# Aligning the programs of ACT and DVE to 128 rows, in an add and GELU kernel

## The chip, the cores and the metric

The kernel runs on one NeuronCore of one Trainium2 chip. The metric is the device time of one execution in microseconds (us), median of several runs, with a granted clock of 1.0. Each run also lists its span, the time from the first to the last instruction that the trace records. Time and span are not the same: the time takes in something that the span does not, and the difference of the two, 2.2 us here, is "the time outside the span".

Engines: in the traces SP issues all 11 DMA transfers; POOL (GpSimd), DVE (VectorE) and ACT (ScalarE) compute, with 19, 35 and 34 instructions. "Row" is one instruction of one engine's program.

## The reference

```python
x, y: 1024 x 4096 float32
z = x + y
out = 0.5 * z * (1 + np.tanh(np.sqrt(2 / np.pi) * (z + 0.044715 * z ** 3)))
```

The kernel computes the second line as z * sigmoid(2 * sqrt(2/pi) * (z + 0.044715 z^3)).

## The kernel before

Each of 128 partitions holds 32,768 elements of z. They are loaded in 4 pieces of x and 4 of y, computed in 16 chunks of 2,048, and stored in 3 pieces.

```python
loads = [8192, 8192, 8192, 8192]
stores = [16384, 10240, 6144]
...
add(c):  POOL (DVE for c = 0)   z = z + y
sq(c):   ACT   w = Square(root * z)          # w in PSUM
stt(c):  DVE   w = (w + c1) * z
sig(c):  ACT   w = Sigmoid(w)
mul(c):  DVE   z = w * z
```

Two helpers edit the finished program. One moves the first two loads ahead of the barrier of all engines with which the program begins; the other makes only POOL wait for the last store at the end, after two closing barriers.

```python
def begin_early(nc, count):
    ...
    at = next(k for k, i in enumerate(head.instructions) if i.engine == SP and isinstance(i, mybir.InstDrain))
    for k, i in enumerate(moved):
        body.instructions.remove(i)
        head.instructions.insert(at + k, i)
...
    tc.compile()
    begin_early(nc, 2)
    wait_late(nc)
```

In the trace of the kernel before, the first row of ACT and of DVE is a drain (at 0.13 and 0.12 us, 8 and 10 ns long), their part in the first barrier; the rows of a program are counted from there. ACT has 55 such rows and DVE 45.

Of the kernel before, what the change touches and what calls it, by code (L numbers as in the profile page):

```python
# [10 lines left out]
def begin_early(nc, count):  # L11


    blocks = nc.main_func.blocks
    head, body = blocks[0], blocks[1]
    SP = mybir.EngineType.SP
    queue = [i for i in body.instructions if i.engine == SP]
    moved = [i for i in queue if isinstance(i, mybir.InstDMACopy)][:count]
    assert not any(i.sync_info and i.sync_info.on_wait for i in moved)
    at = next(k for k, i in enumerate(head.instructions) if i.engine == SP and isinstance(i, mybir.InstDrain))  # L20
    for k, i in enumerate(moved):
        body.instructions.remove(i)
        head.instructions.insert(at + k, i)


def wait_late(nc):


    body, end = nc.main_func.blocks[1:3]
    SP, POOL = mybir.EngineType.SP, mybir.EngineType.Pool  # L30
    last = [i for i in body.instructions if isinstance(i, mybir.InstDMACopy)][-1]
    (sem,) = [u.id for u in last.sync_info.on_update]
    all_done = end.instructions[0]
    clear = next(i for i in end.instructions if isinstance(i, mybir.InstDrain) and i.is_reset_sema)
    assert all_done.engine == SP and clear.engine == POOL and clear.sync_info is None
    waits = all_done.sync_info.on_wait
    its = [w for w in waits if w.id == sem]
    assert len(its) == 1
    rest = [w for w in waits if w.id != sem]

    def drain(old, waits, **reset):
        return mybir.InstDrain(
            name=old.name, engine=old.engine, debug=old.debug,
            sync_info=mybir.SyncInfo(on_wait=waits, on_update=[]), **reset
        )

    at = end.instructions.index(clear)
    clears = [
        drain(
            clear, its, is_reset_sema=True,  # L50
            reset_range_start=clear.reset_range_start, reset_range_stop=clear.reset_range_stop,
        ),
        end.instructions[at + 1],
    ]
    assert isinstance(clears[1], mybir.InstISA) and clears[1].engine == POOL
    del end.instructions[at : at + 2]
    end.instructions[0] = drain(all_done, rest, is_reset_sema=False)
    end.instructions.extend(clears)
# [3 lines left out]
def kernel(  # L62
# [14 lines left out]
    nc = tc.nc  # L77
# [144 lines left out]
    tc.close()  # L222
    tc.compile()  # L223
    begin_early(nc, 2)
    wait_late(nc)


# [28 lines left out]
```

## Time and profile before

| | kernel before |
|---|---|
| time, median of 6 runs | 121.09 us (121.03 to 121.23) |
| span | 118.9 us |
| time outside the span | 2.2 us |
| data in and out | 50.33 MB, DMA queue busy 98.6% |
| first data, last data | 1.02 us, 118.25 us |
| busy DVE, ACT, POOL | 62%, 51%, 59% |

The 16 DMA engines carry data 98.6% of the time, so the end of the span follows the last data. Each transfer is 128 packets of equal size and completes in 16 parts, taken here as one for each DMA engine; the trace records when each part completes. For the last store all 16 completed between 118.33 and 118.69 us. The part that is furthest behind sets the end: it completed at 118.69 us, and the last two rows of the trace, POOL's, follow at 118.71 and 118.82 us.

One line of the timeline, the first add on DVE, which waits for the first loads (start, duration, engine, line, operation, shapes, and the wait before it):

```profile
21.84 2.29 DVE L145 TENSOR_TENSOR z<-z,y 128x2048 f32<-128x2048 f32 x1 [20.44 <-DMA y<-in_y_dram]
```

### The profile page before, as it was taken

The numbers are of one execution on the slowest core, as the hardware profiler recorded it, in microseconds if no ns is written. First come the engines' busy times: TensorE is split into PE (matmuls) and PEld (weight loads), VectorE is DVE, ScalarE is ACT, GpSimd is POOL, SyncE is SP. The second block draws the span as 40 slices with busy tenths as digits, with TensorE's granted clock in tenths as the row PEclk, the third lists the DMA queues.
The fourth block names the chain that finished last, engine by engine and source line by source line (L and its number), as shares of the span: only waits on it lengthen the run. The fifth ranks groups of instructions, "written<-read, shape, count | busy, mean of one in ns | idle before, by whom it ended". The sixth has DMA issues, their size and how long they took to land.

```text
span 118.9 us, 170 instructions
## 1 busy us (share of the span) xinstructions
DVE 73.7 (62%) x35; ACT 61.0 (51%) x34; POOL 69.7 (59%) x19
## 2 busy tenths in 40 slices
DVE  0000000635799995749999958999994999990000
ACT  4000000064888865197698657888829769800000
POOL 0000000699995199999959999959999990000000
DMA  7989898989999898989899998998898889999996
GB/s 254 452 364 518 353 529 353 518 364 474 408 430 452 364 518 353 529 353 518 364 474 408 408 474 353 529 529 353 353 683 375 353 353 441 441 441 441 397 397 265
DMA packets 1584, 50.33 MB, mean 423 GB/s; under 512 B 176, under 2 KB 176, under 8 KB 176
## 3 DMA queue, kind: packets, MB, share of 16 engines
q1 hardware_dynamic: 1584, 50.33, 98.6%
HBM read 33.55 MB, written 16.78 MB: 423 GB/s over the span
## 4 chain that ended last, share of the span: by engine, by line
DMA 51%; POOL 26%; POOLq 4%; DVE 4%; DVEq 2%; ACT 2%; issue 0%; SPq 0%
DMA y<-in_y_dram 51%; POOL z L145 26%; POOLq L223 4%; DVE w L156 2%; DVEq L223 2%; DVE z L168 2%; ACT w L150 2%; SPq L121 0%; POOLq L145 0%
## 5 line engine op out<-in xcount | busy, mean ns | idle before, releaser
L145 POOL TENSOR_TENSOR z<-z,y 128x2048 f32<-128x2048 f32 x15 | 69.4, 4661 | 28.2 <-DMA y<-in_y_dram 28.2
L150 ACT ACTIVATE w<-z 128x2048 f32<-128x2048 f32 x16 | 30.1, 1882 | 37.6 <-DVE z L145 21.4
L156 DVE SCALAR_TENSOR_TENSOR w<-w,z 128x2048 f32<-128x2048 f32 x16 | 36.7, 2295 | 11.2 <-ACT w L150 11.0
L168 DVE TENSOR_TENSOR z<-w,z 128x2048 f32<-128x2048 f32 (+1 forms) x17 | 35.9, 2155 | 0.0
L161 ACT ACTIVATE w<-w 128x2048 f32<-128x2048 f32 x16 | 29.7, 1855 | 4.4 <-DVE w L156 4.3
L145 DVE TENSOR_TENSOR z<-z,y 128x2048 f32<-128x2048 f32 x1 | 2.3, 2292 | 20.4 <-DMA y<-in_y_dram 20.4
L208 ACT ACT_TABLE_LOAD x1 | 1.3, 1283 | 1.3 <-PEq L240 1.3
L207 DVE MEMSET one<- 128x1 f32 x1 | 0.1, 59 | 1.3 <-PEq L240 1.3
L240 POOL MEMSET const-float32-0.0<- 128x1 f32 x1 | 0.1, 99 | 0.2 <-issue 0.2
L208 ACT ACTIVATE one<-one 128x1 f32<-128x1 f32 x1 | 0.2, 203 | 0.0
L240 POOL MEMSET const-bfloat16-1.0<- 128x1 bf16 x1 | 0.1, 101 | 0.0
L240 POOL MEMSET const-uint8-127<- 128x1 uint8 x1 | 0.1, 101 | 0.0
L240 POOL MEMSET const-float32-1.0<- 128x1 f32 x1 | 0.1, 98 | 0.0
## 6 DMA issues: line engine op xcount, KB each, us to landing
z<-in_x_dram SPq DMA_DIRECT2D x4, 4096.0 KB, 31.3
y<-in_y_dram SPq DMA_DIRECT2D x4, 4096.0 KB, 22.2
out_dram<-z SPq DMA_DIRECT2D x1, 5120.0 KB, 15.8
out_dram<-z SPq DMA_DIRECT2D x1, 3072.0 KB, 11.9
out_dram<-z SPq DMA_DIRECT2D x1, 22.0
```

Of the source, the lines that this page charges most:

```text
L145: eng.tensor_add(out=zt[:, a:b], in0=zt[:, a:b], in1=yt[s][:, o : o + b - a])
L150: nc.scalar.activation(out=wt[c], in_=zt[:, a:b], func=act.Square, scale=root)
L156: nc.vector.scalar_tensor_tensor(out=wt[c], in0=wt[c], scalar=c1, in1=zt[:, a:b], op0=alu.add, op1=alu.mult)
L161: nc.scalar.activation(out=wt[c], in_=wt[c], func=act.Sigmoid)
L168: ins = nc.vector.tensor_mul(out=zt[:, a + o : a + o + n], in0=wt[c][:, o : o + n], in1=zt[:, a + o : a + o + n],)
L207: nc.vector.memset(one, 0.0)
L208: nc.scalar.activation(out=one, in_=one, func=act.Sigmoid)
L223: tc.compile()
L240: nc = _bacc.Bacc("TRN2", target_bir_lowering=False, num_devices=1)
```

## The change

The trace of the kernel before has six packets of kind "instruction", of 8,192 bytes each, 11.3 to 8.5 us ahead of the span. I read them as parts of the engines' programs, and call such a packet a fetch; what it holds is not shown. The alignment of the diff is to 128 rows. A "block" below is such a run of 128 rows, a "slot" the place of one row in it, a "border" the place between two of them. That a packet brings just such a block is not shown. A program that starts in the middle of a block may run over a border. The change pads the programs of ACT and DVE so that each begins at a border, to keep the whole program within one block.

```diff
+def align_start(nc):
+    head = nc.main_func.blocks[0].instructions
+    tail = nc.cur_bb.bb.instructions
+    for eng in (nc.scalar, nc.vector):
+        eng.addr_align(128)
+        ins = tail.pop()
+        at = next(
+            k for k, i in enumerate(head)
+            if i.engine == ins.engine and isinstance(i, mybir.InstDrain)
+        )
+        head.insert(at, ins)
...
     begin_early(nc, 2)
+    align_start(nc)
     wait_late(nc)
```

## The prediction

> **What bounds the kernel now.** I read the page first, then the DMA queue by stretches, then the timeline of the start and the waits of the SP queue. The page gives the transfers the whole span:
>
> ```profile
> DMA  7989898989999898989899998998898889999996
> ...
> q1 hardware_dynamic: 1584, 50.33, 98.6%
> ...
> z<-in_x_dram SPq DMA_DIRECT2D x4, 4096.0 KB, 31.3
> y<-in_y_dram SPq DMA_DIRECT2D x4, 4096.0 KB, 22.2
> ```
>
> The busy digits of the 16 DMA engines hardly leave 8 to 9 from the first slice to the last but one, and the queue's packets fill 98.6% of the engines' time. 50.33 MB is 3 x 16.78 MB: x in, y in, the result out, each once, so no byte can be saved by a change like this. By stretches (columns: window and length, busy time of DVE, ACT and POOL with instruction counts, clock, DMA share, GB/s) the first and last two rows are:
>
> ```profile
> 0.00:1.02 1.02, 0.00 (x0) 0.00 (x0) 0.20 (x4) 1.00 0.00 0
> 1.02:11.00 9.98, 0.06 (x1) 1.49 (x2) 0.00 (x0) 1.00 1.04 420
> ...
> 109.00:118.30 9.30, 0.00 (x0) 0.00 (x0) 0.00 (x0) 1.00 0.95 409
> 118.30:118.90 0.60, 0.00 (x0) 0.00 (x0) 0.00 (x0) 1.00 0.00 0
> ```
>
> Nothing moves in the first 1.02 us (SP issues the first load at 0.00, data follows about 1.02 us later), then data flows until about 118.3 us, then 0.6 us of completion and clearing. So the span of 118.9 us is 1.0 + 117.3 + 0.6, and the middle term is 50.33 MB at 429 GB/s. The timed 121.06 us has another 2.2 us outside the span. The chain of waits on the page names POOL for 26%, but it ends with the last multiply at 106.7 us, before the last store; it is not what sets the end. What sets it is whether the queue ever runs dry. It does not: the last load's data is in at 80.0 us and the first store was issued at 77.3; that store is in at about 99.3 and the second was issued at 95.7; that one is in at 111.4 and the third was issued at 106.8. The slacks are 2.7, 3.6 and 4.6 us.
>
> The start is where the change acts:
>
> ```profile
> 0.00 0.38 SPq L121 DMA_DIRECT2D z<-in_x_dram  x1
> ...
> 0.43 0.42 SPq L128 DMA_DIRECT2D y<-in_y_dram  x1
> 1.26 1.28 ACT L208 ACT_TABLE_LOAD   x1 [1.26 <-PEq L240]
> 1.26 0.33 SPq L121 DMA_DIRECT2D z<-in_x_dram  x1
> 1.33 0.06 DVE L207 MEMSET one<- 128x1 f32 x1 [1.33 <-PEq L240]
> ```
>
> The two first loads go out before the barrier of all engines, which releases at about 1.2 us; the third load is the first thing on SP after it. ACT and DVE then do tiny set-up work and wait for data:
>
> ```profile
> DVE z L145 <- DMA y<-in_y_dram: 20.4, 1, 20.4
> ACT w L150 <- DVE z L145: 21.4, 1, 21.4
> ```
>
> [...] its packet records hold six packets of kind "instruction" of 8,192 bytes[...]. They took 455 to 549 ns each and all ran 11.3 to 8.5 us ahead of the span. The windows view of that time shows them (12 GB/s in 4 us is 49 KB) and none between them and the start:
>
> ```profile
> -12.00:-8.00 4.00, 0.00 (x0) 0.00 (x0) 0.00 (x0) 1.00 0.05 12
> -8.00:-1.00 7.00, 0.00 (x0) 0.00 (x0) 0.00 (x0) 1.00 0.00 0
> -1.00:0.00 1.00, 0.00 (x0) 0.00 (x0) 0.00 (x0) 1.00 0.00 0
> ```
>
> In the span the packet records hold no instruction packet. [...]
>
> **The change part by part.** It removes nothing. It adds one alignment per program (ACT, DVE), ahead of the drain with which the engine enters the first barrier; the listing of the two programs shows one more row on each of the two engines and no other row moved. Rows of POOL, SP and PE are the same.
>
> (1) Padding. The alignment has to skip up to 127 slots. [...] the event semaphores of this trace took 17 ns on ACT and 21 ns on DVE[...]. Where SP runs several in a row they start some 60 ns apart (107.155 and 107.219 us). So 127 of them are 2.2 to 2.7 us at the least and 127 x 0.06 = 7.6 us at the most; on average half. ACT and DVE pad at the same time. An estimate, for the real number of slots is not in the trace.
>
> (2) What that delays. The barrier would release at up to 1.2 + 7.6 = 8.8 us, and with it the third load, the table load (1.28 us) and the memset. The third load needs to be out 1.02 us before the first two are through, at 21.7 us: slack 21.7 - 1.02 - 1.26 = 19.4 us. ACT's first work is at 24.2 us, and table load plus first activation are 1.5 us: it could begin them at 22. DVE's first add waits for data until 21.8. All of 7.6 us lies beside the first two loads, so its cost on the path is 0.
>
> (3) Fetches. [...] Two packets of about 0.54 us: if before 1.02 us, free; if later, 0.54 us on one DMA engine, or 1.1 if both fall on the same one. The 16 parts of the last store complete between 118.33 and 118.69 us, so up to 0.36 us may hide. Cost 0 to 1.1 us, mean about 0.2 with the chance that I give it.
>
> (4) Gain. If in the kernel before a program crosses a block border, the crossing would show as an idle stretch not explained by a semaphore. The list of waits has one "issue" entry of 0.2 us and none for ACT or DVE, so inside the span there is nothing to win. In the 2.2 us outside it, the clearing code after the kernel might have sat in another block; a gain of some tenths is possible there and can't be seen in this trace.
>
> Sum: 0 + 0 + 0.2 - 0.15, about 121.1 us.
>
> **The rivals.** A: nothing to be seen, since the padding hides under the first loads and the fetches under the launch; for it speaks the 19.4 us of slack and the absence of instruction packets in the span; 121.0 to 121.2 us. B: fetches move into the stream and push back a DMA engine; for it, the engines have no idle time to absorb 0.5 us; against, 8 KB of 50 MB is nothing if the engine concerned is not the last; 121.3 to 122.1 us. C: a stall at the crossing or in the closing code goes away; for it, someone took the trouble of this change; against, no unexplained wait in the trace; 120.2 to 120.9 us. D: [...] ACT or DVE hold up the barrier beyond 20 us, the queue runs dry before the third load; a microsecond for each microsecond over; against, a fetch took half a microsecond[...]; over 124 us, 2 or 3 in 100.
>
> **Range and chances.** A gets about 60 in 100, B 22, C 15, D 3. 8 in 10 lie between 120.5 and 121.9 us, the point at 121.1. Faster by over 2% would need 2.4 us, more than all the time of the span without data[...]: 2 in 100. Slower by over 2% is D: 3 in 100.
>
> **What would show it.** Padding right: the barrier's release, the third load and the table load start 1 to 8 us later than 1.26, with the start of the first add still near 21.8 us. Hidden right: DMA share unchanged in every stretch and the last data near 118.3. Fetch right or wrong: instruction packets of 8,192 bytes inside the span (B) or ahead of it (A). Gain: the time shrinks more than the span does (C). I am wrong if the first data comes later than about 1.0 us after the span's start, for then the padding delays SP itself; or if the time outside the span, 2.2 us, grows with the padding[...].

Where the text is marked as cut, it told how instructions are fetched and how a DMA engine serves its queues, which no trace of this case had shown, or leaned on that alone; so rival D stands without its cause. jump_first, below, has a cut of the same kind. 0 for the padding, 0 for what it delays, 0.2 for the fetches and -0.15 for the gain, on the 121.06 us of the kernel before, come to about 121.1 us. The terms for padding and fetches are estimates: that a no-operation costs what an event semaphore of the trace does (17 ns on ACT, 21 ns on DVE, some 60 ns from start to start on SP), and that a packet of the length seen ahead of the span (up to 0.549 us) pushes one DMA engine back by that length, weighted with a chance. The 0.15 is a guess: no measured number stands behind it.

## The result, and the profile after

The changed kernel takes 121.49 us, median of 6 runs (121.35 to 121.56); the kernel before 121.09 us. The ratio is 1.003 with a 95% interval of 1.0017 to 1.0043: within 2%, and slower by 0.2 to 0.4%, as the interval leaves out 1. Ratios here are the mean time of one kernel's fast runs over that of the other's of the same rounds, so not quite the ratio of the medians.

The span grew more than the time did: from 118.9 to 119.65 us (median of the 6 runs), while the time outside the span fell from 2.18 to 1.84 us. (These are medians of the differences run by run; 2.18 is from the 9 runs of the kernel before that stood beside the first batch below.) So two effects of opposite sign hide in the 0.4 us: +0.75 - 0.34 = +0.41.

The padding is in the trace, as 63 no-operations on each engine, some 39 ns (ACT) and 47 ns (DVE) from one start to the next (14 and 18 ns long). The columns are line, engine, operation and count, shortest, median and longest duration in ns, and the first and last start in us:

```profile
L31 DVEq NOP  x63: 18/18/18, 0.1 to 3.0; - x63
L31 ACTq NOP  x63: 14/14/14, 0.1 to 2.5; - x63
```

63 places to the border means that the drain stood at slot 128 - 63 = 65 of its block before. The timeline of the start, and of the first add:

```profile
3.87 1.28 ACT L222 ACT_TABLE_LOAD   x1 [3.87 <-PEq L255]
3.88 0.33 SPq L135 DMA_DIRECT2D z<-in_x_dram  x1
...
22.59 2.29 DVE L159 TENSOR_TENSOR z<-z,y 128x2048 f32<-128x2048 f32 x1 [18.59 <-DMA y<-in_y_dram]
```

The barrier, the table load and the third load are late by 2.6 us, for the padding (and, as is shown further below, for a short stall behind it). The first add is late too, by 0.75 us, though it waits for loads that were issued ahead of all this, at the same 0.00 and 0.43 us. The list of DMA queues has a queue that the page before did not have (queue, kind: packets, MB, share):

```profile
q1 hardware_dynamic: 1584, 50.33, 98.0%
q14 instruction: 2, 0.02, 0.0%
```

Two instruction packets are in the span now. The packet records date them: 8,192 bytes each, at 6.57 and 6.61 us, 0.31 us long. From the first load on, two of the sixteen parts of each transfer are late, and stay late:

```
completion of the 16 parts, us   first load (x)                 last store
before                           11.71 to 12.05                 118.33 to 118.69
after                            14 parts 11.53 to 12.01,       14 parts 118.17 to 118.65,
                                 then 12.59 and 12.78           then 119.21 and 119.45
```

The same is seen at the end of the data by stretches (window and length, busy time of DVE, ACT and POOL, clock, DMA share, GB/s). First the kernel before, then the changed one:

```profile
118.00:118.30 0.30, 0.00 (x0) 0.00 (x0) 0.00 (x0) 1.00 0.02 0
```

```profile
118.00:118.30 0.30, 0.00 (x0) 0.00 (x0) 0.00 (x0) 1.00 0.21 82
```

A packet is counted in the window where it begins. Before, no data packet begins after 118.0 us; after, one does (82 GB/s in 0.3 us is 24.6 KB, one packet of the last store), and it ends at 119.12 us, ahead of the latest part at 119.45.

### The profile page after: what moved, and what is told of

The parts are those of the page before. It is cut to its first block, busy times and chain, and to the rows that moved or that the text cites. A ratio compares the mean times of both kernels' runs of the same rounds, so it can differ in the third digit from the quotient of the medians.

```text
span 119.7 us, 296 instructions
## 1 busy us (share of the span) xinstructions
DVE 73.7 (62%) x35; ACT 61.0 (51%) x34; POOL 69.7 (58%) x19
## 4 chain that ended last, share of the span: by engine, by line
DMA 49%; POOL 26%; POOLq 4%; DVE 4%; DVEq 2%; ACT 2%; issue 0%; SPq 0%
DMA y<-in_y_dram 49%; POOL z L159 26%; POOLq L237 4%; DVE w L170 2%; DVEq L237 2%; DVE z L182 2%; ACT w L164 2%; SPq L135 0%; POOLq L159 0%
## 6 DMA issues: line engine op xcount, KB each, us to landing
y<-in_y_dram SPq DMA_DIRECT2D x4, 4096.0 KB, 22.6
```

## The experiments

**Theory.** (a) Where an engine crosses a border, a fetch follows (in the changed kernel the drains behind the border start at 2.9 us on ACT and 3.5 us on DVE, the packets at 6.57 and 6.61 us, so the drains did not wait for these). Where it falls in the stream of data, one DMA engine is pushed back and the whole kernel ends later (two parts 0.6 and 0.8 us behind the others at the first load above). (b) "Closing code" below is what an engine may still run behind its own last row; it has no records in the traces, and that it is part of the time is assumed. In the kernel before, by the count of rows, ACT crossed a border there, and this cost the 0.34 us outside the span; the change moves the crossing to the start, where engines wait anyway (DVE 20.4 us for its first data). **Rivals.** The 2.6 us of delay at the start is what costs; the start on a block is what gains; each engine contributes half of each effect.

The sixteen parts help to tell a fetch from other noise: where a fetch is in the span, one part is late from some moment on, in most of these traces by 0.3 us or more behind the next latest. (Without a fetch the 16 stood 0.3 to 0.6 us apart at the last store, the latest at most 0.2 us behind the next.) The sign is not always there: with ACT at slot 0 and DVE at 75, below, one packet came and the latest part is only 0.15 us behind the next. So the packet records count first. "Outside" is the time less the span, in all the runs of an experiment.

### One engine at a time

The edits of this section and the next are against the changed kernel.

```diff
-    for eng in (nc.scalar, nc.vector):
+    for eng in (nc.scalar,):        # act_only
+    for eng in (nc.vector,):        # dve_only
```

> Alignment on ACT alone. Theory (two effects): the block fetch inside the stream pushes back one DMA engine by 0.6 to 0.9 us, which lengthens the span from 118.9 to about 119.5 to 119.7, one instruction packet in the span; the time outside the span (2.2 us before, 1.8 after) falls by 0.4 only when no engine crosses a block border in the closing code, so DVE still crosses there and it stays 2.2: 121.7 to 121.9 us, slower than the change as a whole. Rival (each engine gives half of both effects): span 119.3, outside 2.0, 121.3 us.

> Alignment on DVE alone. Theory: as for ACT alone, span 119.5 to 119.7, ACT still crosses in the closing code, outside 2.2, 121.7 to 121.9 us. Rival (one engine alone carries the gain outside the span, it being DVE): span 119.6, outside 1.8, 121.4 us, and ACT alone 121.8.

| | time, median of 5 | ratio (95%) | span | outside | late parts |
|---|---|---|---|---|---|
| before (9 runs) | 121.07 | | 118.9 | 2.18 | none |
| ACT alone | 121.18 | 1.0012 (0.9998 to 1.0025) | 119.3 | 1.85 | one, by 0.3 to 0.5 |
| DVE alone | 121.84 | 1.0061 (1.0047 to 1.0074) | 119.6 | 2.21 | one, by 0.6 to 0.7 |
| both, the change | 121.49 | 1.003 | 119.65 | 1.84 | two |

My expectation for ACT alone was wrong. I had thought that each engine crosses in the closing code and that the gain comes only with both. The whole gain outside the span is ACT's; DVE's alignment has no gain at all and the larger loss. Neither engine gives half of both effects, so that rival falls as well. The losses don't add up: with both there are two late parts, so, as parts are taken here, the two fetches fall on different DMA engines, and the later one decides. (The profile of DVE alone fell on its longest run, 122.11 us, in which the other 15 parts of the last store are late together by some 0.5 us as well; the lag in the table is that behind these 15, and the span is the median of the runs.) In each of the two traces one instruction packet is in the span, at 6.61 us; this is the line of ACT alone:

```profile
q14 instruction: 1, 0.01, 0.0%
```

### The padding without its delay

```diff
-        eng.addr_align(128)
+        eng.addr_align(128, max_nops=0)     # jump_over: the engine branches over the padding
```

and for jump_first, besides, the alignment goes ahead of each engine's first row instead of its drain.

> Both engines, same place, but the loader branches over the padding in place of 63 no-operations on each. Theory: the barrier comes back to about 1.5 to 1.9 us, outside stays 1.8; the fetches are asked for 2.5 to 3 us earlier but still meet the first load's data (from 1.0 us on), so the span stays near 119.6: 121.4 us. Rival (the padding's delay of the third load is what costs): span 118.9, 120.7 us.

> Both engines, branch over the padding, and the alignment ahead of the register set-up, the engine's first instructions. Theory: [...] the fetches run before or just as the data starts, so no DMA engine is pushed back: span 118.9, outside 1.8, 120.7 us, faster than both kernels. If the fetches still land after 1.0 us: span 119.5, 121.3 us. Rival (crossing ahead of the set-up delays SP's start or the clock of the time): 121.1 us or more with no packet in the stream.

The kernel before stands at the same 121.07 us (one batch with the two above). jump_over took 121.49 us (ratio 1.0037, 1.0024 to 1.005), span 119.7, outside 1.85; jump_first 121.47 us (ratio 1.0034, 1.0021 to 1.0047), span 119.6, outside 1.85. In jump_over the third load is out at 1.25 us, as in the kernel before, and the two fetches are still there:

```profile
1.25 0.33 SPq L135 DMA_DIRECT2D z<-in_x_dram  x1
```

```profile
q14 instruction: 2, 0.02, 0.0%
```

So the delay of 2.6 us at the start costs nothing: without it the time is the same. The rival falls, and the step of the prediction that hid the padding under the first loads holds. jump_first was my hope for a kernel faster than both, by having the fetches come before the data starts, at 1.0 us; it missed. Its packets came at 3.11 and 4.19 us, as late as the 3.03 and 4.17 us of jump_over. The traces show why: ACT takes its branch at 0.12 us and DVE at 0.10 us in both, and the next row in both is the drain (ACT's at 0.57 and 0.55 us). Nothing lies between, for the compiler drops the set-up rows, as the next batch shows. As far as the traces tell, jump_first is jump_over once more, and an earlier fetch has not been tried.

### Four runs that measured the noise

Four kernels were meant to move the border with plain no-operations (12 at the end of ACT, 40 at the start of DVE, 70 on PE to delay the barrier alone) or by taking out ACT's unused set-up rows. Their edits are against the kernel before.

```diff
+    put_nops(nc, nc.scalar, 2, 12)     # act_tail: eng.nop() x12 ahead of ACT's closing drain
+    put_nops(nc, nc.vector, 0, 40)     # dve_mid
+    put_nops(nc, nc.tensor, 0, 70)     # pe_nops
+    lean_start(nc)                     # act_lean: 6 set-up rows of ACT removed
```

> The kernel before, with no alignment; ACT's six set-up rows (register moves and a base load that its program never uses) are taken out, so that its program ends six slots earlier. Theory: ACT alone holds the 0.35 us outside the span, because it crosses a block border in the closing code that is timed, some 8 rows in; DVE, ten rows shorter, crosses later and that costs nothing. If six rows are enough to move ACT's crossing out of the timed part: span 118.9 with no instruction packet in it, outside 1.85, 120.75 us, faster than both kernels. If six are not enough: 121.07. Rival (the gain outside the span comes from the ACT program starting on a block, not from where the border falls): 121.07.

> The kernel before plus 12 no-operations on ACT behind its last activation, ahead of the closing barriers, near 104 us. Theory: the border is now crossed at the end of ACT's own program, where it waits for SP anyway; outside the span 1.85, but one fetch runs beside the last store and pushes back one DMA engine by some 0.4 us: span 119.3, 121.2 us, as with the alignment of ACT alone. Rival (start on a block): outside stays 2.2 and the time is 121.1 to 121.5.

> The kernel before plus 40 no-operations at the start of DVE, so that the border falls in the middle of its program (23 rows after the drain). Theory: one instruction packet near 50 to 60 us, span about 119.6, outside 2.2, 121.8 us, as with the alignment of DVE alone: a fetch anywhere in the stream costs the same 0.6 to 0.8. Rival (the 2 to 3 us of delay at the start is what pushes the DMA back): here the delay is 1.9 us and the packet lies elsewhere; the lag would be there from the first load on.

> The kernel before plus 70 no-operations on the idle PE ahead of its part in the first barrier: the barrier and the third load are late by 2.5 to 3.5 us as in the changed kernel, but ACT and DVE cross no border. Theory: the delay hides under the first two loads: no instruction packet in the span, span 118.9, 121.07 us. Rival (the delay costs): span 119.3 to 119.7, 121.5 us.

All four missed what they were made for. The traces show no no-operations, and the barrier at 1.2 us as ever; they have the 55 rows of ACT and 45 of DVE that the kernel before has. The compiler drops such rows, and had dropped the set-up rows all along. So, as far as the traces show, these are the kernel before run four times again, and that has its own use: medians 121.17, 121.12, 121.12 and 121.47 us beside 121.18, outside 2.17 to 2.20 in all, but single runs from 121.0 to 121.77. The profile of pe_nops shows what such a long run is: span 119.6, no instruction packet, and all 16 parts of the last store late together (119.04 to 119.37 us). That slowing is not a fetch; what it is stays open. A single run that differs by 0.6 us proves nothing here; medians, the time outside the span and the single late part do.

### The border put where I want it

An alignment with an offset survives the compiler. It puts the drain at a chosen slot, and the border then falls 128 - slot rows behind the drain. The edits are against the changed kernel.

```diff
-    for eng in (nc.scalar, nc.vector):
-        eng.addr_align(128)
+    for eng, slot in ((nc.scalar, 73),):                     # act_slot73
+    for eng, slot in ((nc.vector, 105),):                    # dve_slot105
+    for eng, slot in ((nc.scalar, 0), (nc.vector, 75)):      # act_0_dve_75
+        eng.addr_align(128, offset=slot)
```

> The compiler drops plain no-operations and unused set-up rows, so the four kernels of the last batch were the kernel before once more; an alignment with an offset survives. The changed kernel's 63 no-operations put the drain of ACT and DVE at slot 65 of a block of 128 before; ACT has 55 rows from there, so its program ends at slot 119 and it crosses the border 8 rows into the closing code; DVE has 45 and crosses 18 rows in. Here ACT's drain is put at slot 73 (8 no-operations), DVE is untouched: the border falls just behind ACT's own last row, at about 112.2 us, 6.5 us before the end. Theory (border in the closing code costs 0.35, wherever the program starts): outside the span 1.85 in place of 2.2; the fetch comes near 114 to 116 us beside the last store and costs 0 to 0.4: 120.7 to 121.1 us. Rival (the gain needs the program to start on a block, or the closing code is only shorter because of the fetch before the stream): outside 2.2, 121.1 us or more.

> DVE's drain at slot 105 (40 no-operations), ACT untouched: the border falls 23 rows into DVE's program, near 50 to 65 us. Theory (a fetch in the stream costs the same anywhere): one instruction packet some 3 us after that row, one DMA engine late from then on and not before, span 119.5 to 119.7, outside 2.2, 121.7 to 121.9 us. Rival (what costs is the delay of 1.9 us at the start, or a fetch only beside the first loads): lag from the first load on, or none and 121.1 us.

> ACT on a block of its own as in the change, DVE's drain at slot 75, ten slots later than before, so that DVE crosses the border 8 rows into the closing code, where ACT did before. Theory (the place in the closing code decides, whichever engine): outside the span back to 2.2 though ACT starts on a block, one packet in the span, span 119.3: 121.5 us. Rival (only ACT's closing code is on the timed path): outside 1.85, 121.15 us.

The traces confirm the slot 65 that was inferred above: 8, 40 and 10 no-operations were added to reach 73, 105 and 75. Of the first two:

```profile
L31 ACTq NOP  x8: 14/14/14, 0.1 to 0.4; - x8
```

```profile
L31 DVEq NOP  x40: 18/18/18, 0.1 to 1.9; - x40
```

| | border behind, by the count of rows | time, median | ratio (95%) | span | outside | instruction packet |
|---|---|---|---|---|---|---|
| before (11 runs) | ACT: row 8 of closing code; DVE: row 18 | 121.07 | | 118.9 | 2.18 | none |
| ACT at 73 | ACT's own last row | 120.98 | 0.9984 (0.9966 to 1.0001) | 119.1 | 1.84 | 117.05 us |
| DVE at 105 | row 23 of DVE | 122.01 | 1.0071 (1.0048 to 1.0094) | 119.8 | 2.19 | 69.60 us |
| ACT at 0, DVE at 75 | DVE: row 8 of closing code | 121.46 | 1.0024 (1.0002 to 1.0045) | 119.2 | 2.25 | 6.52 us |

DVE at slot 105 shows that a fetch in the middle of the stream costs as one at its start does. The 16 parts of the first load are together (11.65 to 12.10 us), so the padding, 1.9 us here, pushed nothing back. Row 23 (the drain is row 0) starts at 67.85 us, the packet follows at 69.60, and from then on one part is late: the last load's parts are in by 80.07 us but for one at 80.75, the last store's by 118.72 but for one at 119.38. The last part is 0.7 us later than in the kernel before, and its lag, 0.66 us, is that of DVE alone (0.6 to 0.7). The median of the runs lost 0.9 us; the rest is of the size of the noise just described, and the interval is wide.

ACT at slot 73 gets the whole gain outside the span though its program starts on no block; that rival falls. And ACT at 0 with DVE at 75 loses the whole gain though ACT starts on a block; by the count of rows, DVE now crosses where ACT did. Outside the span these runs go with the place of the border, counted from the engine's own last row, whichever engine it is: 2.18 to 2.25 us where ACT or DVE has it 8 rows behind, 1.84 and 1.85 us where DVE has it 18 rows behind and ACT has it right behind its last row or not at all (ACT at 73, ACT alone), 1.84 us where neither has one (the change). So 8 rows in costs 0.3 to 0.4 us, 18 rows in nothing. The crossing itself is not seen there; it is concluded from these differences.

A crossing at the start is seen, though, and it fits. These are the drains of the changed kernel, just behind the border, and after them two that follow padding within a block (ACT of act_slot73, DVE of dve_slot105):

```profile
L255 ACTq DRAIN  x1: 132/132/132, 2.9 to 2.9; - x1
L255 DVEq DRAIN  x1: 134/134/134, 3.5 to 3.5; - x1
```

```profile
L255 ACTq DRAIN  x1: 8/8/8, 0.5 to 0.5; - x1
```

```profile
L255 DVEq DRAIN  x1: 10/10/10, 2.0 to 2.0; - x1
```

From the start of the last no-operation to the start of the drain the instruction records have 362 ns on ACT and 481 ns on DVE across the border, and 52 and 65 ns within a block. So the border held ACT up for some 0.31 us and DVE for 0.42 us, 3 us and more before the instruction packet. The time outside the span changed by 0.34 us for ACT's crossing (2.18 to 1.84) and 0.41 us for DVE's (1.84 to 2.25). That the crossing in the closing code is the same stall is thus likely, by its size on both engines, but not seen. Why 18 rows in it costs nothing is open.

ACT at slot 73 is also the first kernel below the one before: the fetch comes at 117.05 us, up to 5 us behind the border, and costs 0.2 us of span in place of the 0.4 of ACT alone (one part of the last store at 118.88 us, the others by 118.61). With ACT at 0 and DVE at 75 ACT's fetch costs 0.3 us. What sets this size is not settled. The gain of 0.09 us is at the edge of what the runs can tell.

### The border without a fetch

The last run moves ACT's border the other way, out of the costly part of the closing code, by a shorter program: 46 rows in place of 55, so that the border is 17 rows into the closing code if the program still starts at slot 65. The edit is against the kernel before; the lines with # put cut code in words.

```diff
+def shorten(nc, sqs, muls):
+    # the first barrier, and the second of the two closing ones, on all engines
+    ...
+    for c in (2, 6, 10, 14):
+        # the wait of sq(c) on POOL moves to mul(c - 2), which sq(c) waits for
+    # sq(0) no longer waits for the load that add(0) has waited for
```

> No alignment anywhere. ACT's program is made nine rows shorter than in the kernel before (46 in place of 55; DVE 45 as before): two barriers that the argument does not need are taken out (the first, and the second of the two at the end), four of ACT's waits on POOL move to the DVE multiply that ACT waits for anyway, and one wait on a load that DVE has already made is dropped. ACT then crosses the block border 17 rows into the closing code, next to where DVE crosses it (18) without being seen in the time. Theory: outside the span 1.85, no instruction packet in the span, span 118.9: 120.7 us, faster than both kernels and than ACT at slot 73. Rival (the closing code's border costs at row 17 too, or on ACT at any row): outside 2.2, 121.1 us. The moved waits delay four multiplies by 0.3 us beside the stream, which should cost nothing.

It took 121.0 us, median of 5, beside 121.17: ratio 0.9982 (0.9969 to 0.9996), faster than both kernels by a little. No packet of 8,192 bytes is in its span (the one packet of the instruction queue there has 32 bytes), and the median span is 119.0, as that of the kernel before in the same rounds; its profile fell on the longest of its runs, 121.27 us. Outside is 1.98 us, only 0.2 below the 2.17 beside it and not at 1.85. The direction is as expected, but 0.13 of the expected 0.32 us is missing. Since this kernel also drops barriers, which changes the very start and end of the measured time, this run doesn't tell whether the border still costs something 17 rows in.

## Why the prediction was right, and where it was not

- **What bounds the kernel**: right. The two terms of data and of what lies before the first of it and behind the last account for the whole span after as well, and what grew is the last data's time (118.25 to 119.12 us), not the wait for the first (1.02 and 1.00 us).
- **(1) Padding**: right. 63 slots, near the half of 127 that was supposed, at 39 and 47 ns; 2.5 and 3.0 us, inside the bounds given. Not foreseen was the stall at the border behind it, 0.31 and 0.42 us, which hides as well.
- **(2) What it delays**: right that the late barrier is free, as jump_over shows. But the sign that was named for it, a first add still at 21.8 us, failed: it came at 22.59, for the fetch and not for the padding (in jump_over, which has the packets and not the delay, DVE idles 21.2 us behind its memset, to 22.6 us).
- **(3) Fetches**: what was named came, and the size was wrong. The text had it as one of two cases, "Two packets of about 0.54 us", and entered a mean of 0.2 us. It happened, and cost 0.75 us of span. Two errors are in that. The chance was set too low: the alignment puts a border ahead of the drain of both engines, so a crossing at the start was part of the change, and six instruction packets ahead of the span were in the trace. And the lag was taken to be the packet's length less up to 0.36 us that may hide: it is 0.3 to 0.5 us for ACT's packet and 0.6 to 0.7 for DVE's, each of 0.31 us, with the engine aligned alone. In the changed kernel nothing of it hid; ACT's fetch alone cost 0.2 to 0.4 us of span, by where it fell. Why the lag is longer than the packet, and not the same for both, is not settled.
- **(4) Gain**: the place was right, the size too small. Entered at 0.15 us; measured 0.34 us, in the closing code as suspected. The sign named for a crossing, idle time that no semaphore explains, is right too: it stands between the padding and the drains of the changed kernel (0.31 and 0.42 us). That it is ACT's alone (outside 1.85 us with ACT aligned alone, 2.21 with DVE) was not foreseen; by the count of rows only ACT crossed as early as 8 rows into that code.
- **The sum**: 0.2 - 0.15 stood for what measured 0.75 - 0.34. The point of 121.1 us was low by 0.4; the rivals B and C were set against each other and came both, while A, given 60 in 100, did not happen. That the time still lies inside the range owes something to luck: the two terms were each about a quarter to a half of what they measured, and they have opposite signs.

## What to carry to other kernels

In this kernel, which the DMA engines bound (busy 98.6%), one instruction packet of 0.31 to 0.39 us on one of them cost 0.2 to 0.9 us of span (medians of the runs). It came late: 1.8 us after the start of the first row behind the border (67.85 to 69.60 us, DVE at 105), 3.7 and 3.1 us after it (the drains of ACT and DVE, each aligned alone), and 5 us after the end of ACT's own rows (112.1 to 117.05 us, ACT at 73). In such a kernel, keep block borders out of the stream of data, by the length of the program or by its place in the block. Look also at what the time holds beyond the span; the 0.34 us put down here to a border in the closing code showed in no profile. Split a small net effect by engine and by time inside and outside the span before explaining it, and see in the trace that an edit has survived the compiler.
